# Seven block products for every fourth pair of row tiles in an MLP's second product

## The chip, the cores and the metric

The kernel runs on one core of one Trainium2 chip. The metric is the device time of one execution in microseconds (us). The engines are TensorE (PE in the profile; its weight loads PEld), VectorE (DVE), ScalarE (ACT), GpSimd (POOL) and SyncE (SP), which issues the DMAs. "fp32r" is the form in which TensorE takes 32-bit floats.

## The reference

One layer of an encoder over 256 tokens of width 2048: attention (GQA and MLA heads), attention to 256 memory tokens, and a squared-ReLU MLP, each followed by a layer norm of a scaled residual. What the change touches is the MLP at the end:

```python
def squared_relu_mlp(h, w_mlp_in, w_mlp_out):          # h (1, 256, 2048)
    return jnp.square(jax.nn.relu(h @ w_mlp_in)) @ w_mlp_out   # 2048 -> 8192 -> 2048
...
ff = squared_relu_mlp(x, w_mlp_in[l], w_mlp_out[l])
x = layer_norm(ALPHA * x + ff, ln3_g[l], ln3_b[l])
```

## The kernel before, in words

**Precision by three products.** Each operand is split into a high part (rounded, a copy on ScalarE, line 79) and a low part (the rest, a subtraction on VectorE, line 80), and a product is the sum of three matmuls: high x high, high x low, low x high (`mm3`, lines 144 to 147). `split` does this for weights and for activations alike.

**Weights.** A `Stream` takes a weight matrix in tiles of 1 MB: a buffer `raw` of 128 x 2048 (pool `rawp`, three buffers) is filled by one DMA from SP (line 133), and each half of it (1024 columns) is split into `w_hi` and `w_lo` (pool `wsp`, four buffers of each). After each half, `pump` issues a piece of waiting side work from the deque `side`.

**The MLP** (lines 703 to 760) walks over the 8192 hidden rows in NCH = 4 chunks of CH = 16 row tiles of 128. In a chunk:

- Four groups (`hidden_group`) of G = 4 row tiles make the hidden rows. The weights are the stationary operand and the tokens (`x2t`) move, so the result comes out transposed, rows by tokens. High weights multiply high and low tokens in one matmul of 512 columns (line 194), low weights the high tokens in one of 256 (line 199). A group reads eight halves, that is four `raw` tiles, and writes four PSUM banks, `acc` (pool `psA`, four banks) and `att` (pool `psT`, four banks) in turn. `hidden` (lines 706 to 712) adds the two halves of a bank, squares what is positive, and splits it into `ht`, which holds 16 tiles, each 256 high and 256 low columns.
- Then four column groups of 512 (`proj_tokens` on `s_mo`): for each of 16 tiles and each of two blocks of 128 tokens, one `mm3` with `ht` stationary and the weights moving. Each column group uses two banks, from `acc` for n = 0 and 1, from `att` for n = 2 and 3. At its end VectorE adds each bank to the rows of the residual, `res` (lines 755 and 758), and in the last chunk takes the statistics for the layer norm.
- The last column group of the last chunk has its weights split ahead into two wide buffers (`last_weights`, line 714) and runs token block by token block, so that the norm of the first block lies beside the matmuls of the second.

**Order.** The program is written in the order above, and the Tile framework's scheduler lays out each engine's queue at compile time; an instruction may go out ahead of earlier ones of the program when its inputs and its buffer are ready. Buffers are asked for by pool and name (`raw`, `w_hi`, `tmp`, `acc`). `big` is a pool of three buffers of 128 x 8192; in the MLP they hold `x2t`, and `ht` in turn, and the first group's weights, split early.

Of the kernel before, what the change touches and what calls it, by code (L numbers as in the profile page):

```python
# [11 lines left out]
F32 = mybir.dt.float32  # L12
F32R = mybir.dt.float32r
# [5 lines left out]
P = 128  # L19
# [19 lines left out]
def encoder_kernel(ctx: ExitStack, tc: tile.TileContext, t, out):  # L39
# [6 lines left out]
    midp = ctx.enter_context(tc.tile_pool(name="midp", bufs=1))  # L46
    resp = ctx.enter_context(tc.tile_pool(name="resp", bufs=2))
    tmp = ctx.enter_context(tc.tile_pool(name="tmp", bufs=7))
    ptp = ctx.enter_context(tc.tile_pool(name="ptp", bufs=2))
    small = ctx.enter_context(tc.tile_pool(name="small", bufs=6))  # L50
    psA = ctx.enter_context(tc.tile_pool(name="psA", bufs=4, space=bass.MemoryType.PSUM))
    psT = ctx.enter_context(tc.tile_pool(name="psT", bufs=4, space=bass.MemoryType.PSUM))

# [23 lines left out]
    def split(hi, lo, src, scale=None, pinned=False):  # L77
        if scale is None:
            pin(nc.scalar.activation(hi, src, AF.Copy), pinned)  # L79
            return pin(nc.vector.tensor_tensor(out=lo, in0=src, in1=f(hi), op=ALU.subtract), pinned)  # L80
# [413 lines left out]
    def stats_tile():  # L494
        return [small.tile([P, 5, 6], F32, tag="bn", name="bn"), 0]
# [210 lines left out]
    def hidden(ps, ht, j):  # L706
# [5 lines left out]
        split(ht[:, j, 0:S], ht[:, j, S:2 * S], lo)  # L712

    def last_weights(k):

        hi, lo = wide_w[0][:, k * 512:(k + 2) * 512], wide_w[1][:, k * 512:(k + 2) * 512]
        u, h = divmod(k, 4)
        if h == 0:
            wide_w[2] = raw_tile()
            nc.sync.dma_start(wide_w[2], t["w_mo"][s_mo.ap.shape[0] - 4 + u])  # L720
        split(hi, lo, wide_w[2][:, h * 512:(h + 2) * 512])
        return hi, lo

    G = 4

    def hidden_group(nexts, tiles, ht, j0):
# [7 lines left out]
        for i in range(G):  # L734
            hidden(outs[i], ht, j0 + i)

    for c in range(NCH):
        ht = big3(f"ht{c}")
        for g in range(CH // G):
            first = c == 0 and g == 0  # L740
            hidden_group((lambda k: w_mi0[k // 2]) if first else (lambda k: s_in.next()),
                         att_tile if g % 2 else acc_tile, ht, g * G)
            if first:
                side.extend(residual("ln2"))
        for n in range(4):
            tiles = att_tile if n >= 2 else acc_tile
            if c == NCH - 1 and n == 3:
                wide_w = [big.tile([P, 8192], F32R, tag="big", name=f"w{i}") for i in range(2)] + [None]
                ps = proj_tokens(None, ht, CH, 512, by_block=True, wide=last_weights, tiles=tiles)
            else:  # L750
                ps = proj_tokens(s_mo, ht, CH, 512, by_block=False, tiles=tiles)
            for b, o, w, p_ in ps:
                r = res[b][:, n * 512 + o:n * 512 + o + w]
                if c == 0:
                    nc.vector.scalar_tensor_tensor(out=r, in0=r, scalar=ALPHA, in1=p_[:, :w],
                                                   op0=ALU.mult, op1=ALU.add)
                else:
                    nc.vector.tensor_tensor(out=r, in0=r, in1=p_[:, :w], op=ALU.add)
                if c == NCH - 1:
                    stats(sts[b], r)  # L760

    g3, b3 = raw_tile(), raw_tile()
# [44 lines left out]
def _layout(i):  # L807
    f32 = np.float32
    a = {}
    x = np.asarray(i["x"])[0]  # L810
    a["x"] = x
    a["xT"] = np.ascontiguousarray(x.T.reshape(4, 4, P, S).transpose(0, 2, 1, 3)).reshape(4, P, 4 * S)
    a["mem"] = np.asarray(i["mem"])[0]
    w = np.asarray(i["w_in"])[0]
    qa, ka, va, cq, ckv, kr = np.split(w, np.cumsum([1024, 256, 256, 512, 512]), axis=1)
    a["w_qa"] = _rows(_pairs(qa, DH), 4, 512)
    a["w_ka"] = _rows(_pairs(ka, DH), 8, 256)
    a["w_vkr"] = _rows(np.concatenate([va, _pairs(kr, ROPE)], axis=1), 4, 320)
# [34 lines left out]
    a["w_mo"] = np.concatenate([_rows(mo[c * CH * P:(c + 1) * CH * P], 4, 512) for c in range(NCH)])  # L853
# [42 lines left out]
```

## Time and profile before

| | |
|---|---|
| median of 3 runs | 1123.22 us (1122.05 to 1123.25) |
| the profiled execution | 1123.25 us, of which the span from first to last instruction 1121.4 us |
| matmuls, TensorE busy | 6004, 1105.5 us (99%) |
| VectorE busy, ScalarE busy, GpSimd busy | 729.0 us (65%), 537.0 us (48%), 38.2 us (3%) |
| mean granted TensorE clock | 0.998 |
| DMA | 215.85 MB, mean 192 GB/s |
| the MLP's share | weights for the hidden rows and for the second product: 64 transfers of 1 MB each |

A row of a timeline reads: start in us from the start of the span, duration in us, engine, line of the kernel, operation, output <- inputs, count; in brackets the idle time of the engine ahead of it and who ended it. A row of the groups reads: line, engine, operation, output <- inputs, shapes, count | busy us in total, mean ns of one | idle us of the engine ahead of them and who ended it.

### The profile page before, as it was taken

The numbers are of one execution on the slowest core, as the hardware profiler recorded it, in microseconds if no ns is written. First come the engines' busy times: TensorE is split into PE (matmuls) and PEld (weight loads), VectorE is DVE, ScalarE is ACT, GpSimd is POOL, SyncE is SP. The second block draws the span as 40 slices with busy tenths as digits, with TensorE's granted clock in tenths as the row PEclk, the third lists the DMA queues.
The fourth block names the chain that finished last, engine by engine and source line by source line (L and its number), as shares of the span: only waits on it lengthen the run. The fifth ranks groups of instructions, "written<-read, shape, count | busy, mean of one in ns | idle before, by whom it ended". The sixth has DMA issues, their size and how long they took to land.

```text
span 1121.4 us, 15079 instructions
## 1 busy us (share of the span) xinstructions
PE 1105.5 (99%) x6004; PEld 954.2 (85%) x6004; DVE 729.0 (65%) x1036; ACT 537.0 (48%) x778; POOL 38.2 (3%) x45
## 2 busy tenths in 40 slices
PE   9999999999999989999999999999999999999996
PEld 6988899888998878888888888888888888888885
DVE  5878677687788677854545565555556454665575
ACT  6555565546576344543344454334444333544440
POOL 1402000000100000000000000000000000000000
PEclk9999999999999999999999999999999999999999
DMA  9664454476467426655555555555555555555562
GB/s 336 224 225 151 150 188 150 151 240 239 162 224 262 150 75 225 204 205 193 188 189 189 188 186 192 195 198 177 208 188 188 193 188 188 188 188 188 191 259 76
DMA packets 37942, 215.85 MB, mean 192 GB/s; under 512 B 4336, under 2 KB 5232, under 8 KB 14192
## 3 DMA queue, kind: packets, MB, share of 16 engines
q1 hardware_dynamic: 37872, 214.89, 54.6%
q8 instruction: 47, 0.77, 0.3%
q14 instruction: 23, 0.19, 0.1%
HBM read 212.78 MB, written 2.10 MB: 192 GB/s over the span
## 4 chain that ended last, share of the span: by engine, by line
PE 96%; DMA 2%; DVE 1%; ACT 0%; issue 0%; SPq 0%; POOL 0%; DVEq 0%; ACTq 0%
PE acc L146 12%; PE acc L145 12%; PE acc L147 12%; PE acc L194 11%; PE att L194 11%; PE att L147 6%; PE att L145 6%; PE att L146 6%; PE acc L199 5%; PE att L199 5%; PE acc L187 2%; PE acc L185 2%; PE acc L186 2%; PE att L534 1%; PE att L349 1%; DMA raw<-in_w_ka 1%
## 5 line engine op out<-in xcount | busy, mean ns | idle before, releaser
L80 DVE TENSOR_TENSOR w_lo<-raw,w_hi 128x1024 fp32r<-128x1024 f32 (+2 forms) x374 | 444.6, 1193 | 327.4 <-ACT w_hi L79 326.3
L79 ACT ACTIVATE w_hi<-raw 128x1024 fp32r<-128x1024 f32 (+2 forms) x374 | 386.5, 1036 | 459.0 <-PE acc L147 171.0
L194 PE MATMUL att<-x2t,w_hi 128*128 128x512 f32 x512 | 139.6, 394 | 0.0
L194 PE MATMUL acc<-x2t,w_hi 128*128 128x512 f32 x480 | 130.9, 394 | 0.0
L145 PE MATMUL acc<-w_hi,ht 128*128 128x512 f32 x256 | 99.6, 389 | 0.0
L146 PE MATMUL acc<-w_lo,ht 128*128 128x512 f32 x256 | 99.6, 389 | 0.0
L147 PE MATMUL acc<-w_hi,ht 128*128 128x512 f32 x256 | 99.6, 389 | 0.0
L194 PEld LDWEIGHTS att<-x2t,w_hi 128*128 128x128 f32 x512 | 88.1, 189 | 12.3
L194 PEld LDWEIGHTS acc<-x2t,w_hi 128*128 128x128 f32 x480 | 82.5, 189 | 11.5
L146 PE MATMUL att<-w_lo,ht 128*128 128x512 f32 x224 | 87.1, 389 | 0.0
L147 PE MATMUL att<-w_hi,ht 128*128 128x512 f32 x224 | 87.1, 389 | 0.0
L145 PE MATMUL att<-w_hi,ht 128*128 128x512 f32 x224 | 87.0, 389 | 0.0
L199 PEld LDWEIGHTS att<-x2t,w_lo 128*128 128x128 f32 x512 | 77.5, 189 | 10.2
L199 PEld LDWEIGHTS acc<-x2t,w_lo 128*128 128x128 f32 x480 | 72.6, 189 | 9.5
L199 PE MATMUL att<-x2t,w_lo 128*128 128x256 f32 x512 | 80.2, 281 | 0.0
L199 PE MATMUL acc<-x2t,w_lo 128*128 128x256 f32 x480 | 75.1, 281 | 0.0
L146 PE MATMUL acc<-w_lo,xt 128*128 128x512 f32 (+2 forms) x192 | 69.5, 363 | 0.2 <-DVE w_lo L80 0.2
L147 PE MATMUL acc<-w_hi,xt 128*128 128x512 f32 (+2 forms) x192 | 69.1, 361 | 0.0
L145 PE MATMUL acc<-w_hi,xt 128*128 128x512 f32 (+2 forms) x192 | 66.1, 364 | 1.0 <-ACT w_hi L79 1.0
L147 PEld LDWEIGHTS acc<-w_hi,ht 128*128 128x128 f32 x256 | 48.0, 188 | 10.0
L145 PEld LDWEIGHTS acc<-w_hi,ht 128*128 128x128 f32 x256 | 48.0, 188 | 10.0
L146 PEld LDWEIGHTS acc<-w_lo,ht 128*128 128x128 f32 x256 | 48.0, 188 | 10.0
(221 smaller groups left out, 1738.1 us busy)
## 6 DMA issues: line engine op xcount, KB each, us to landing
raw<-in_w_mi SPq DMA_DIRECT2D x64, 1024.0 KB, 4.8
raw<-in_w_mo SPq DMA_DIRECT2D x64, 1024.0 KB, 4.8
raw<-in_w_out SPq DMA_DIRECT2D x16, 1024.0 KB, 4.9
raw<-in_w_b SPq DMA_DIRECT2D x5, 1024.0 KB, 4.8
raw<-in_w_qa SPq DMA_DIRECT2D x16, 256.0 KB, 5.4
raw<-in_w_qa SPq DMA_DIRECT2D x4, 1024.0 KB, 4.9
raw<-in_w_ckv SPq DMA_DIRECT2D x4, 1024.0 KB, 5.1
raw<-in_w_cq SPq DMA_DIRECT2D x4, 1024.0 KB, 4.8
```

What stands on the lines that cost most here:

```text
L79: pin(nc.scalar.activation(hi, src, AF.Copy), pinned)
L80: return pin(nc.vector.tensor_tensor(out=lo, in0=src, in1=f(hi), op=ALU.subtract), pinned)
L145: nc.tensor.matmul(ps, ah, bh, start=start, stop=False)
L146: nc.tensor.matmul(ps, ah, bl, start=False, stop=False)
L147: nc.tensor.matmul(ps, al, bh, start=False, stop=stop)
L185: nc.tensor.matmul(ps, hi, xt[:, k, 0:S], start=k == 0, stop=False)
L186: nc.tensor.matmul(ps, hi, xt[:, k, S:2 * S], start=False, stop=False)
L187: nc.tensor.matmul(ps, lo, xt[:, k, 0:S], start=False, stop=k == nk - 1)
L194: nc.tensor.matmul(ps, hi[:, i * P:(i + 1) * P], xt[:, k, :], start=k == 0, stop=k == nk - 1)
L199: nc.tensor.matmul(ps[:, 0:S], lo[:, i * P:(i + 1) * P], xt[:, k, 0:S], start=False, stop=False)
L349: nc.tensor.transpose(pp[:, st * S + b * P:st * S + b * P + P], ev[:, b, st * P:(st + 1) * P], ident)
L534: nc.tensor.transpose(ps[:, o:o + P], x(b, k // 4)[:, (k % 4 + j) * P:(k % 4 + j + 1) * P], ident)
```

## The change

The second product is now made in blocks: two column groups at a time (half q of the 2048 columns), all 16 row tiles of the chunk, both token blocks. So a chunk has two blocks, each with four `acc` banks x11, x12, x21, x22 (token block, column group) and, new, four `att` banks p1, p5, p6, p7. The row tiles go in eight pairs p. Three pairs of four are multiplied as before: 2 tiles x 2 token blocks x 2 column groups x 3 matmuls. For p = 3 and p = 7, the 2 x 2 blocks (tokens by row tiles, row tiles by columns) are multiplied by the Strassen-Winograd scheme with seven products in place of eight. For that

- `hidden` also forms four sums of 128 x 128 blocks of hidden values, on VectorE, and splits them (`sums_h`);
- `load_unit` loads the weights of a pair (1 MB as before, laid out so that the four blocks lie side by side), and for p = 3 and 7 puts three additions on VectorE (`sums_w`) on `side`. Units of p = 0, 1, 4, 5 lie in `raw` buffers, the others in the third `big` buffer (`wx`), whose use becomes possible since `ht` is now one buffer for all chunks. Units are asked for two ahead; the first two of a chunk just before its last hidden group;
- at the end of a block the seven products are put together in `res`: four additions of the x banks, four with the p banks, and four more on VectorE (q = 0) or GpSimd (q = 1), and one copy on ScalarE.

The second half of the columns in the last chunk stays as it was. The pools `midp` and `ptp`, no longer needed there, are closed ahead of the MLP to make room for `sums_h`.

```diff
-    s_in, s_mo = Stream(t["w_mi"][4:]), Stream(t["w_mo"])
+    early.close()
+    late = ctx.enter_context(tc.tile_pool(name="late", bufs=1))
+    s_in = Stream(t["w_mi"][4:])
     sts = [stats_tile() for _ in range(NB)]
+    ht = big3("ht")
+    sums_h = late.tile([P, 2048], F32R, name="sums_h").rearrange("p (u l c) -> p u l c", l=2, c=512)
+    wx = big.tile([P, 8192], F32, tag="big", name="wx")
+    raw2, sums_w = [[wx[:, o:o + 2048] for o in (i, i + 2048)] for i in (0, 4096)]
...
+    def hidden(ps, j):
+        r = []
+        for i in range(2):
+            r.append(square(ps[i]))
+            split(ht[:, j + i, 0:S], ht[:, j + i, S:2 * S], r[i])
+        if strassen(j // 2):
+            (a11, a21), (a12, a22) = [(x[:, 0:P], x[:, P:S]) for x in r]
+            s = tmp_tile()
+            s1, s2, s3, s4 = [s[:, o:o + P] for o in range(0, 4 * P, P)]
+            for o, a, b, op in ((s1, a21, a22, ALU.subtract), (s3, a11, a21, ALU.subtract),
+                                (s2, s1, a11, ALU.subtract), (s4, a12, s2, ALU.add)):
+                nc.vector.tensor_tensor(out=o, in0=a, in1=b, op=op)
+            split(sums_h[:, j // 8, 0, :], sums_h[:, j // 8, 1, :], s)
+
+    def strassen(p):
+        return p % 4 == 3
...
+    def load_unit(chunk):
+        if not units or units[0][0] != chunk:
+            return
+        c, q, p = units.pop(0)
+        seven = strassen(p)
+        raw = raw_tile() if p % 4 < 2 else raw2[p % 4 - 2]
+        nc.sync.dma_start(raw, t["w_mo"][(c * 2 + q) * (CH // 2) + p])
+        s = None
+        if seven:
+            s = sums_w[p // 4 % 2]
+            b12, b22, b21 = [raw[:, o:o + 512] for o in (0, 1024, 1536)]
+            def add(out, a, b):
+                side.append(lambda: nc.vector.tensor_tensor(out=out, in0=a, in1=b, op=ALU.add))
+            add(s[:, 0:1024]..., raw[:, 512:1536]..., b12[:, None, :].broadcast_to([P, 2, 512]))
+            add(s[:, 1024:1536], s[:, 0:512], b22)
+            add(s[:, 1536:2048], s[:, 1024:1536], b21)
+        loaded.append((raw, s))
...
+    def pair_product(c, q):
+        x11, x12, x21, x22 = [acc_tile() for _ in range(4)]
+        p1, p5, p6, p7 = [att_tile() for _ in range(4)]
+        n = CH // 2
+        for p in range(n):
+            load_unit(c)
+            raw, s = loaded.popleft()
+            k = 2 * p
...
+            if strassen(p):
+                first, last = p == 3, p == n - 1
+                pump(len(side))
+                for src, todo in ((raw[:, 512:1536], ((p1, a(k, 0), first), (x12, sm(3), False))),
+                                  (raw[:, 1536:2048], ((x11, a(k + 1, 0), False),)),
+                                  (s[:, 0:1024], ((p5, sm(0), first), (p7, sm(2), first))),
+                                  (s[:, 1024:2048], ((p6, sm(1), first), (x21, a(k + 1, 1), False)))):
+                    for (hi, lo), (ps, (ah, al), start) in zip(part(src), todo):
+                        mm3(ps, ah, al, hi, lo, start, last)
+            else:
+                for i in range(2):
+                    w = part(raw[:, i * 1024:(i + 1) * 1024])
+                    for (hi, lo), to in zip(w, ((x12, x22), (x11, x21))):
+                        for b in range(2):
+                            ah, al = a(k + i, b)
+                            mm3(to[b], ah, al, hi, lo, p == 0 and i == 0, to[b] is x22 and p == n - 2 and i == 1)
...
+        rest = nc.gpsimd if q == 1 else nc.vector
+        first_add(r22, x22)
+        m1 = tmp_tile()
+        nc.scalar.activation(m1, p1, AF.Copy)
+        first_add(r12, x12)
+        first_add(r11, x11)
+        add(r12, r12, p5)
+        add(r22, r22, p5)
+        u3 = tmp_tile()
+        u2 = tmp_tile()
+        add(u2, m1, p6)
+        add(u3, u2, p7)
+        first_add(r21, x21)
+        add(r11, r11, m1, eng=rest)
+        add(r12, r12, u2, ALU.subtract, rest)
+        add(r21, r21, u3, eng=rest)
+        add(r22, r22, u3, ALU.subtract, rest)
...
     for c in range(NCH):
-        ht = big3(f"ht{c}")
         for g in range(CH // G):
             first = c == 0 and g == 0
+            if g == CH // G - 1:
+                load_unit(c)
+                load_unit(c)
             hidden_group((lambda k: w_mi0[k // 2]) if first else (lambda k: s_in.next()),
-                         att_tile if g % 2 else acc_tile, ht, g * G)
+                         att_tile if g % 2 else acc_tile, g * G)
...
-        for n in range(4):
-            tiles = att_tile if n >= 2 else acc_tile
...
+        for q in range(2):
+            if c < NCH - 1 or q == 0:
+                pair_product(c, q)
+                continue
```

`part` splits 512 or 1024 columns of a source into `w_hi` and `w_lo` and pumps one piece of side work; `first_add(r, ps)` adds a bank to the residual rows (scaled by ALPHA in the first chunk).

More of the change, by code (lines that the diff above doesn't have):

```diff
@@ L724, in encoder_kernel, with hidden_group @@
     G = 4
-    def hidden_group(nexts, tiles, ht, j0):
+    def hidden_group(nexts, tiles, j0):
         outs = [tiles() for _ in range(G)]
@@ L733, in hidden_group @@
                           x2t, k + i, KT)
-        for i in range(G):
-            hidden(outs[i], ht, j0 + i)
+        for i in range(0, G, 2):
+            hidden(outs[i:i + 2], j0 + i)
+    units = [(c, q, p) for c in range(NCH) for q in range(2) for p in range(CH // 2)
+             if not (c == NCH - 1 and q == 1)]
+    loaded = deque()
+    def load_unit(chunk):
[11 more added lines that the diff above has]
+                side.append(lambda: nc.vector.tensor_tensor(out=out, in0=a, in1=b, op=ALU.add))
+            add(s[:, 0:1024].rearrange("p (i c) -> p i c", i=2), raw[:, 512:1536].rearrange("p (i c) -> p i c", i=2),
+                b12[:, None, :].broadcast_to([P, 2, 512]))
+            add(s[:, 1024:1536], s[:, 0:512], b22)
+            add(s[:, 1536:2048], s[:, 1024:1536], b21)
+        loaded.append((raw, s))
@@ new lines, in part, with a, sm, first_add @@
+    def part(src):
+        w = src.shape[1]
+        hi = wsp.tile([P, 1024], F32R, tag="w_hi", name="w_hi")
+        lo = wsp.tile([P, 1024], F32R, tag="w_lo", name="w_lo")
+        split(hi[:, :w], lo[:, :w], src)
+        pump()
+        return [(hi[:, o:o + 512], lo[:, o:o + 512]) for o in range(0, w, 512)]
+    def pair_product(c, q):
[6 more added lines that the diff above has]
+            k = 2 * p
+            def a(k_, b):
+                return ht[:, k_, b * P:(b + 1) * P], ht[:, k_, S + b * P:S + (b + 1) * P]
+            def sm(i):
+                return (sums_h[:, p // 4, 0, i * P:(i + 1) * P], sums_h[:, p // 4, 1, i * P:(i + 1) * P])
+            if strassen(p):
[14 more added lines that the diff above has]
+                            mm3(to[b], ah, al, hi, lo, p == 0 and i == 0, to[b] is x22 and p == n - 2 and i == 1)
+        cols = [slice((2 * q + i) * 512, (2 * q + i + 1) * 512) for i in range(2)]
+        r11, r12, r21, r22 = [res[b][:, cc] for b in range(NB) for cc in cols]
+        def first_add(r, ps):
+            if c == 0:
+                nc.vector.scalar_tensor_tensor(out=r, in0=r, scalar=ALPHA, in1=ps,
+                                               op0=ALU.mult, op1=ALU.add)
+            else:
+                nc.vector.tensor_tensor(out=r, in0=r, in1=ps, op=ALU.add)
+        def add(o, x, y, op=ALU.add, eng=nc.vector):
+            eng.tensor_tensor(out=o, in0=x, in1=y, op=op)
+        rest = nc.gpsimd if q == 1 else nc.vector
[15 more added lines that the diff above has]
+        add(r22, r22, u3, ALU.subtract, rest)
+        if c == NCH - 1:
+            for b, r in ((0, r11), (0, r12), (1, r21), (1, r22)):
+                stats(sts[b], r)
@@ new lines, in encoder_kernel @@
+        for q in range(2):
+            if c < NCH - 1 or q == 0:
+                pair_product(c, q)
+                continue
+            s_ml = Stream(t["w_ml"])
+            for n in (2, 3):
+                if n == 3:
+                    wide_w = [big.tile([P, 8192], F32R, tag="big", name=f"w{i}") for i in range(2)] + [None]
+                    ps = proj_tokens(None, ht, CH, 512, by_block=True, wide=last_weights, tiles=att_tile)
+                else:
+                    ps = proj_tokens(s_ml, ht, CH, 512, by_block=False, tiles=acc_tile)
+                for b, o, w, p_ in ps:
+                    r = res[b][:, n * 512 + o:n * 512 + o + w]
@@ L852, in _layout @@
     mo = np.asarray(i["w_mlp_out"])[0]
-    a["w_mo"] = np.concatenate([_rows(mo[c * CH * P:(c + 1) * CH * P], 4, 512) for c in range(NCH)])
+    m = mo.reshape(NCH, CH // 2, 2, P, 2, 2, 512)
+    order = [m[:, :, i, :, :, j, :] for i, j in ((0, 1), (0, 0), (1, 1), (1, 0))]
+    m = np.stack(order, axis=4).transpose(0, 3, 1, 2, 4, 5).reshape(NCH * CH, P, 2048)
+    a["w_mo"] = m[:-CH // 2]
+    a["w_ml"] = _rows(mo[-CH * P:, 1024:], 4, 512)
     for n in ("ln1", "ln2", "ln3", "mem_ln"):
```

22 lines of the change are left out of this document (6 added, 16 removed).

## The prediction

> **What bounds the kernel now.** I read the head of the page first (span, engines), then the chain that ended last, then stretches of the MLP and its groups of instructions, because the change lies there.
>
> ```profile
> span 1121.4 us, 15079 instructions
> PE 1105.5 (99%) x6004; PEld 954.2 (85%) x6004; DVE 729.0 (65%) x1036; ACT 537.0 (48%) x778; POOL 38.2 (3%) x45
> PE 96%; DMA 2%; DVE 1%; ACT 0%; issue 0%; SPq 0%; POOL 0%; DVEq 0%; ACTq 0%
> 624.72:647.16 22.44, 22.44 (x130) 19.63 (x128) 13.72 (x21) 10.93 (x17) 0.00 (x0) 1.00 0.53 189
> 669.60:756.50 86.90, 86.90 (x385) 71.97 (x384) 46.71 (x51) 35.91 (x39) 0.00 (x0) 1.00 0.55 190
> 669.60 0.39 PE L145 MATMUL acc<-w_hi,ht 128*128 128x512 f32 x1
> 756.64 1.07 PE L194 MATMUL acc<-x2t,w_hi 128*128 128x512 f32 x4
> L80 DVE TENSOR_TENSOR w_lo<-raw,w_hi 128x1024 fp32r<-128x1024 f32 x350 | 427.3, 1223 | 323.9 <-ACT w_hi L79 323.1
> L79 ACT ACTIVATE w_hi<-raw 128x1024 fp32r<-128x1024 f32 x350 | 370.7, 1061 | 448.2 <-PE acc L147 165.1 <-PE att L147 82.9 <-PE acc L194 82.5
> ```
>
> The profiled execution took 1123.25 us (span 1121.4), the median of the three is 1123.22, so they are the same. TensorE is the chain: 96% of it. The two stretch rows (the first number after the window is its length, then busy time and count of PE, PEld, DVE, ACT, POOL) are a group of hidden rows and a chunk's second product: PE is busy for all of both, at clock 1.00. Behind PE there is slack that waits on PE itself: the weight splits on ScalarE (448.2 us idle, mostly until PE gives back a split buffer) and VectorE. The second product of a chunk runs from 669.60 to 756.64: 16 k x 2 token tiles x 4 column groups x 3 = 384 matmuls, so one costs 87.04/384 = 0.2267 us. A cut of matmuls is worth its full price as long as weights and PSUM banks still come in time.
>
> **The change part by part.** *Fewer matmuls.* The code makes 4 chunks x 2 column halves x 8 pairs, less the last half: 7 blocks, each with two pairs (p = 3 and 7) by seven products. Such a pair needs 7 x 3 = 21 matmuls in place of 24. 14 x 3 x 0.2267 = **9.5 us saved**.
>
> *More work on VectorE, ScalarE, GpSimd.* The prices, and one place where GpSimd adds beside VectorE:
>
> ```profile
> L565 DVE TENSOR_TENSOR res<-res,tmp 128x512 f32<-128x512 f32 x32 | 20.6, 685 | 1.4 <-DMA tmp<-in_ln_g 1.1 <-DMA tmp<-in_ln_b 0.2
> 1066.44 1.28 DVE L758 TENSOR_TENSOR res<-res,acc 128x512 f32<-128x512 f32 x2
> L295 DVE TENSOR_TENSOR tmp<-acc,tab_a 128x128 f32<-128x128 f32 x4 | 1.0, 282 | 0.0
> 32.51 1.30 POOL L297 TENSOR_TENSOR tmp<-tmp 128x512 f32<-128x512 f32 x1 [6.72 <-DVE tmp L295]
> 34.37 4.96 POOL L297 TENSOR_TENSOR tmp<-tmp 128x512 f32<-128x512 f32 x1 [0.55 <-DVE rs_v L88]
> 34.34 3.82 DVE L80 TENSOR_TENSOR w_lo<-raw,w_hi 128x1024 fp32r<-128x1024 f32 x4
> ```
>
> Weight sums: one add of 1024 and two of 512, 1.22 + 2 x 0.68 = 2.6 us a pair, 14 times: 36 us. Splits: 3.5 parts of 1024 in place of 2, so 1.5 x 1.22 x 14 = 26 us on VectorE and 22 us on ScalarE. Sums of hidden rows: 8 times four adds of 128 (0.28 each) and a split of 512 (0.68): 14 us. Results: 12 adds a block in place of 4 (in three blocks four of them go to GpSimd): 44 more x 0.68 = 30 us. VectorE comes to 729 + 106 = 835 us, 74% of the span. Averaged, all of it lies in the idle time of the L80 row, and I cost the weight sums, the hidden sums and the splits at nothing: they are issued two units ahead and the four split buffers let them run 4 parts ahead of PE. The ends of the blocks are another matter (below). GpSimd's 12 adds (1.3 to 5.0 us each) feed rows of the result that are next needed two products later: nothing.
>
> *Loads moved ahead.* As many transfers of 1 MB are issued as before (56 + 8), but the first two units of each chunk are asked for ahead of the last hidden group's four weight tiles, and they sit in two of the three raw buffers until the second product begins. This is the step that I price highest:
>
> ```profile
> 147.87 6.98 SPq L133 DMA_DIRECT2D raw<-in_w_out  x2
> 172.52 4.97 SPq L133 DMA_DIRECT2D raw<-in_w_out  x2
> 191.87 37.49 SPq L133 DMA_DIRECT2D raw<-in_w_out  x7
> 229.41 10.41 SPq L593 DMA_DIRECT2D tmp<-in_mem  x10
> 210.16 0.46 ACT L338 ACTIVATE tmp<-att,nm 128x256 f32<-128x256 f32 x1
> 229.64 0.47 ACT L338 ACTIVATE tmp<-att,nm 128x256 f32<-128x256 f32 x1
> 628.22 0.33 SPq L133 DMA_DIRECT2D raw<-in_w_mi  x1
> 632.44 0.33 SPq L133 DMA_DIRECT2D raw<-in_w_mi  x1
> 638.06 0.33 SPq L133 DMA_DIRECT2D raw<-in_w_mi  x1
> raw<-in_w_mi SPq DMA_DIRECT2D x64, 1024.0 KB, 4.8
> DMA to landing us min/median/max: 3.5/4.8/9.7
> 1070.06 0.33 SPq L720 DMA_DIRECT2D raw<-in_w_mo  x1
> 1074.91 2.01 ACT L79 ACTIVATE w<-raw 128x1024 fp32r<-128x1024 f32 x2 [1.49 <-DMA raw<-in_w_mo]
> 1076.01 2.36 DVE L80 TENSOR_TENSOR w<-raw,w 128x1024 fp32r<-128x1024 f32 x2 [1.33 <-ACT w L79]
> 1078.40 0.33 SPq L720 DMA_DIRECT2D raw<-in_w_mo  x1
> 582.78 0.93 PE acc L194 x4
> ```
>
> Could the scheduler let the group's tiles pass the two units? The first rows speak against it. The mem loads need only a tmp buffer and stand in the program behind the eighth w_out tile, yet eleven (2 + 2 + 7) went out before them; they went at 229.41, beside the last attention exponentials (229.64) that take tmp buffers, though none had taken one since 210.16. So buffers of one name seem to be handed out in program order, and only different names pass each other. Then U0 and U1 take the buffers that come free at 628.22 and 632.44, and the group's first tile goes out at 638.06. From there one buffer turns round: issue 1070.06, data used from 1074.91, both halves split, issued again 1078.40, 8.34 us a turn, with the first half ready 7.1 us after issue (1076.01 + 1.18). A group of 22.44 us eats one tile in 5.61 us. The fourth tile's first half is ready at 638.06 + 3 x 8.34 + 7.1 = 670.2; PE, starting the group at 647.16 (end of the window above), wants its low half, after four high matmuls (0.93), at 647.16 + 3 x 5.61 + 0.9 = 664.9. PE is late by **5.3 us a chunk, 21.2 us for four**. Ends: at the shortest landing (3.5, not 4.85) four landings are 5.4 us shorter and nothing is lost; at transfers half again as slow it is 10 us a chunk. I take 5.3, because 4.8 is the median of 64 such transfers.
>
> *Ends of the blocks.* Before, a product wrote two banks and the next had two others. Now all four acc banks end with the block, x21 with its very last matmul, and the next work writes the same four. Within a block's last pair (21 x 0.2267 = 4.8 us) and up to the second part of the next block (12 matmuls, 2.7 us later) VectorE must do one split left over (1.22), eight adds that empty banks (at 0.64 back to back, the L758 row of two), and two splits (2.44): 8.8 us in 7.5, so 1.3 us late. Four blocks end this way (three first halves, and the last one, ahead of the old product). Where a hidden group follows (three times), bank x21 is wanted at 3 x 0.23 = 0.7 us, and VectorE has emptied it after u2, u3 and the add, 1.2 us if at once, 2.5 us with a split between: 1.2 us late in the mean. 4 x 1.3 + 3 x 1.2 = **8.8 us**. The trace of before has no such end; the bounds are nothing (VectorE takes the reads early, PE does other banks first) and all adds ahead of the next split: 1.22 + 12 x 0.64 + 1.22 = 10.1 us from 4.4 us before the end, 5.5 us late, with eight adds 2.9: 4 x 5.5 + 3 x 2.9 = 31 us. I take the lower value, since in the rows above splits start as soon as ScalarE is done.
>
> GpSimd's adds at three block ends share something with VectorE: the add took 1.30 us alone and 4.96 us while four splits ran, and those four took 3.82 us together, 0.96 each, no more than the 1.22 of the L80 row. The one that waits is GpSimd, so I cost VectorE nothing. The Trainium skill (SBUF — State Buffer, section "SBUF: two separate sides") says that a GpSimd instruction and a VectorE one with two SBUF inputs take one port pair as an exclusive lock, and whichever starts first holds it for its whole length. The trace agrees for GpSimd; by the rule VectorE could be the one that waits, up to 1.3 us for each of four adds, and the sum would be up to 15.6 us higher.
>
> *Kept.* The last half stays as it was; its wide buffers now wait for the block before it instead of the hidden group, which ends some 22 us (one old product) before 1083, while their first data come at 1074.91: nothing.
>
> **Sum:** 1123.25 - 9.5 + 21.2 + 8.8 = **1143.7 us**.
>
> **The rivals.** *A, faster: no starvation.* If weight tiles of the last hidden group pass the two units, or a unit is split early and gives its buffer back, the 21.2 us vanish, and if PE at the block ends does other banks first, half of their price too. For it: the split buffers have slack that a scheduler could use. Against it: the w_out and mem rows. Then 1123.25 - 9.5 + 8.8 / 2 = 1118; it decides when PE's lateness in the last hidden group is under (9.5 - 4.4) / 4 = 1.3 us a chunk. *B, VectorE's order.* All adds ahead of the splits at the block ends: 31 in place of 8.8, 1166. For it, they stand first in the program; against it, they wait for PE one by one, and splits fit between. *C, the lock of the port pair turned against VectorE* at the three ends: 4 x 1.3 x 3 = 15.6, up to 1159. Against it: the four splits at 34.34. *D, the change pays for itself and no more:* landings near 3.5 us leave no starvation, and the block ends take back 8.8 of 9.5: 1122.5, with 1119 to 1127 for a little of either. For it: the shortest landing; against it: the 4.8 is of a stage with one transfer at a time, as here.
>
> **How the numbers follow.** Forecast 0.55 (its own range 1128 to 1160); A 0.19 (0.17 faster, 0.02 no difference); B 0.10; C 0.05; D 0.11 (0.02 faster, 0.06 no difference, 0.03 slower). Faster by over 0.2% (about 2.2 us, what a measurement here can tell from no change) 0.19, within it 0.08, slower 0.73. The range that holds 8 in 10 goes from 1117, to take in most of A and D, to 1160, above C and the upper part of the forecast, without B.
>
> **What would show it.** Right: 42 matmuls fewer in the second product, at 0.227 us start to start; in each chunk's last hidden group, idle PE of some 2.5 us twice, with ACT w_hi waiting for DMA raw<-in_w_mi, and issues of w_mi there 8 us apart instead of 5.6; at the block ends PE waiting 1 to 2 us for DVE res or w_lo; VectorE at 73 to 75%. Wrong: issues of w_mi staying 5.6 us apart there (then A); PE gaps of 5 us at block ends with DVE res first (then B); VectorE's splits stretched beside GpSimd's adds (then C).

## The result, and the profile after

The changed kernel takes 1151.78 us (median of 4 runs, 1148.94 to 1155.82) against 1123.09 us: ratio 1.026, 95% interval 1.0229 to 1.0292, slower. Forecast were 1143.7 us (1117 to 1160) and "slower" with 0.73. The profiled execution took 1151.52 us. First the head of its page and its chain that ended last:

```profile
span 1149.7 us, 15234 instructions
PE 1114.6 (97%) x5962; PEld 951.6 (83%) x5962; DVE 821.7 (71%) x1190; ACT 563.5 (49%) x821; POOL 62.1 (5%) x57
PE 80%; DMA 10%; DVE 5%; ACT 2%; issue 2%; SPq 0%; POOL 0%; ACTq 0%; DVEq 0%; POOLq 0%
```

TensorE does 42 matmuls fewer, as meant, yet is busy 9.1 us *longer* (1114.6 for 1105.5), and the chain, 96% TensorE before, now has 10% DMA and 5% VectorE in it. Two readings follow from this: TensorE waits, and some of its matmuls are slower or drawn out. What it waits for (us in total, times, longest):

```profile
PE att L195 <- ACT w_hi L80: 15.6, 10, 2.9
PE acc L147 <- DVE w_lo L81: 2.2, 4, 0.6
PE acc L200 <- DVE w_lo L81: 1.9, 3, 0.6
```

L195 into att is the matmul of a chunk's last hidden group (and its second); L147 and L200 into acc are the first uses of low weights behind a block's end. Now the stretches, read as the row 624.72 to 647.16 of before: first a chunk's third hidden group, in 22.44 us, then the last groups of the four chunks, from the start of each to the start of its second product.

```profile
447.95:470.39 22.44, 22.44 (x129) 19.63 (x128) 16.64 (x31) 9.43 (x15) 0.00 (x0) 1.00 0.67 229
470.39:501.22 30.83, 25.12 (x117) 20.40 (x116) 15.94 (x23) 11.89 (x18) 0.00 (x0) 0.89 0.37 126
657.68:685.59 27.91, 23.66 (x117) 19.13 (x116) 12.91 (x20) 11.31 (x16) 0.00 (x0) 0.94 0.36 119
842.16:868.45 26.29, 22.90 (x117) 19.02 (x116) 12.91 (x20) 11.29 (x16) 0.00 (x0) 0.94 0.38 127
1025.01:1051.22 26.21, 23.35 (x118) 19.12 (x116) 12.92 (x20) 11.30 (x16) 0.00 (x0) 0.93 0.38 126
```

The last groups are long, by 3.8 to 8.4 us within these stretches, with the DMA share down from 0.67 to 0.37 and the clock (the column ahead of it) at 0.89 to 0.94. That is not the whole loss: the last twelve of a group's 128 matmuls stand behind the first four of the second product, as here in the third chunk:

```profile
868.45 1.07 PE L146 MATMUL acc<-w_hi,ht 128*128 128x512 f32 x4
869.36 1.11 PE L200 MATMUL att<-x2t,w_lo 128*128 128x256 f32 x8
870.32 1.09 PE L195 MATMUL att<-x2t,w_hi 128*128 128x512 f32 x4
```

Counted to the end of its own matmuls (871.25 here, where the next one starts), less the 0.91 us of those four, a group loses 10.3, 7.4, 5.7 and 5.7 us in the four chunks, 29.0 us in all.

Inside the second chunk's group, the requests for weights and ScalarE's splits (start, duration, in brackets the idle time before and who ended it):

```profile
643.16 0.33 SPq L782 DMA_DIRECT2D raw<-in_w_mo  x1
648.59 27.20 SPq L134 DMA_DIRECT2D raw<-in_w_mi  x4
653.52 2.01 ACT L80 ACTIVATE w_hi<-raw 128x1024 fp32r<-128x1024 f32 x2 [6.22 <-DMA raw<-in_w_mi]
663.59 2.01 ACT L80 ACTIVATE w_hi<-raw 128x1024 fp32r<-128x1024 f32 x2 [2.44 <-DMA raw<-in_w_mi]
671.98 2.01 ACT L80 ACTIVATE w_hi<-raw 128x1024 fp32r<-128x1024 f32 x2 [6.37 <-DMA raw<-in_w_mi]
```

The `w_mo` request at 643.16 and one before it hold two of three raw buffers; the four `w_mi` requests go out one by one, the last ending 27.20 us after the first, so (27.20 - 0.33)/3 = 8.96 us a turn on the average. The second turn alone took 10.07 us: its tile was asked for at 657.00 and ScalarE could start on it only 6.6 us later, at 663.59, where the first tile took 4.9 us. The page shows the waits in the idle time of `ACT w_hi`, ended by DMA each time, and one step later as TensorE's wait for `w_hi`.

What the wait leaves behind is seen in the third chunk. TensorE's first matmuls behind a gap (timeline), and three stretches, the first in that gap:

```profile
855.91 2.07 PE L195 MATMUL att<-x2t,w_hi 128*128 128x512 f32 x4 [2.22 <-ACT w_hi L80]
```

```profile
853.69:855.64 1.95, 0.00 (x0) 0.00 (x0) 0.00 (x0) 0.84 (x1) 0.00 (x0) 1.00 0.12 50
855.64:859.05 3.41, 3.14 (x9) 2.67 (x10) 2.36 (x2) 1.16 (x2) 0.00 (x0) 0.50 0.00 0
859.05:862.50 3.45, 3.45 (x20) 3.01 (x19) 0.00 (x0) 0.00 (x0) 0.00 (x0) 1.00 0.87 304
```

Four matmuls take 2.07 us instead of about 1.09. The granted clock is still 1.00 for the first 1.95 us of the gap, 0.50 for the next 3.41 us, then 1.00 again. Five such stretches lie in the last hidden groups. By an estimate (5 x 3.41 / 2) they make 8.5 us of TensorE's extra busy time, which is about half of it: 42 matmuls fewer should have left 1105.5 - 9.5 = 1096.0 us, and `e1_late` below, which has no such stretch in the MLP, is still busy for 1101.7 us.

Last, VectorE at a block's end (second chunk, q = 0), and the wait of TensorE that it makes:

```profile
724.61 0.68 DVE L844 TENSOR_TENSOR res<-res,acc 128x512 f32<-128x512 f32 x1
725.87 1.23 DVE L789 TENSOR_TENSOR wx<-wx 128x1024 f32<-128x1024 f32 x1 [0.58 <-DMA wx<-in_w_mo]
727.01 1.22 DVE L81 TENSOR_TENSOR w_lo<-wx,w_hi 128x1024 fp32r<-128x1024 f32 x1
728.15 0.68 DVE L844 TENSOR_TENSOR res<-res,acc 128x512 f32<-128x512 f32 x1
728.75 0.69 DVE L789 TENSOR_TENSOR wx<-wx 128x512 f32<-128x512 f32 x1
729.35 0.68 DVE L844 TENSOR_TENSOR res<-res,acc 128x512 f32<-128x512 f32 x1
729.95 1.22 DVE L81 TENSOR_TENSOR w_lo<-raw,w_hi 128x1024 fp32r<-128x1024 f32 x1
731.23 0.50 PE L147 MATMUL acc<-w_lo,ht 128*128 128x512 f32 x1 [0.64 <-DVE w_lo L81]
```

The split at 729.95 is the one TensorE needs to open the next block. Two weight sums (L789) of a pair that is multiplied some 17 us later stand ahead of it, and VectorE even idled 0.58 us for the transfer that feeds the first.

### The profile page after: what moved, and what is told of

It reads as the page before. It is cut to its first block, busy times and chain, and to the rows that moved or that the text cites. A ratio compares the mean times of both kernels' runs of the same rounds, so it can differ in the third digit from the quotient of the medians.

```text
span 1149.7 us, 15234 instructions
## 1 busy us (share of the span) xinstructions
PE 1114.6 (97%) x5962; PEld 951.6 (83%) x5962; DVE 821.7 (71%) x1190; ACT 563.5 (49%) x821; POOL 62.1 (5%) x57
## 4 chain that ended last, share of the span: by engine, by line
PE 80%; DMA 10%; DVE 5%; ACT 2%; issue 2%; SPq 0%; POOL 0%; ACTq 0%; DVEq 0%; POOLq 0%
PE acc L147 14%; PE acc L148 14%; PE acc L146 14%; PE acc L195 8%; PE att L195 7%; DMA raw<-in_w_mi 6%; PE acc L200 4%; PE att L200 4%; DVE w_lo L81 3%; PE acc L188 2%; PE acc L186 2%; PE acc L187 2%; DMA wx<-in_w_mo 2%; ACT w_hi L80 2%; PE att L146 2%; PE att L148 2%
## 5 line engine op out<-in xcount | busy, mean ns | idle before, releaser
L81 DVE TENSOR_TENSOR w_lo<-raw,w_hi 128x1024 fp32r<-128x1024 f32 (+2 forms) x318 | 376.7, 1202 | 190.6 <-ACT w_hi L80 184.0
L80 ACT ACTIVATE w_hi<-raw 128x1024 fp32r<-128x1024 f32 (+2 forms) x318 | 321.8, 1030 | 321.7 <-PE acc L148 85.7
L195 PE MATMUL att<-x2t,w_hi 128*128 128x512 f32 x512 | 145.4, 407 | 15.6 <-ACT w_hi L80 15.6
L147 PE MATMUL acc<-w_lo,ht 128*128 128x512 f32 x396 | 155.1, 392 | 1.9 <-DVE w_lo L81 1.9
L148 PE MATMUL acc<-w_hi,ht 128*128 128x512 f32 x396 | 154.2, 389 | 0.0
L80 ACT ACTIVATE w_hi<-wx 128x1024 fp32r<-128x1024 f32 x84 | 82.6, 991 | 134.3 <-PE acc L148 130.6
L81 DVE TENSOR_TENSOR w_lo<-wx,w_hi 128x1024 fp32r<-128x1024 f32 x84 | 94.6, 1136 | 64.7 <-ACT w_hi L80 64.7
L195 PE MATMUL acc<-x2t,w_hi 128*128 128x512 f32 x480 | 133.7, 395 | 0.0
L146 PE MATMUL acc<-w_hi,ht 128*128 128x512 f32 x396 | 130.7, 390 | 0.0
L195 PEld LDWEIGHTS att<-x2t,w_hi 128*128 128x128 f32 x512 | 91.4, 196 | 30.5 <-ACT w_hi L80 17.7
L195 PEld LDWEIGHTS acc<-x2t,w_hi 128*128 128x128 f32 x480 | 82.5, 189 | 12.1 <-DVE res L844 0.5
L200 PEld LDWEIGHTS att<-x2t,w_lo 128*128 128x128 f32 x512 | 79.7, 196 | 15.0 <-DVE w_lo L81 5.2
L147 PEld LDWEIGHTS acc<-w_lo,ht 128*128 128x128 f32 x396 | 74.3, 188 | 20.6 <-DVE w_lo L81 5.3
L146 PEld LDWEIGHTS acc<-w_hi,ht 128*128 128x128 f32 x396 | 74.3, 188 | 15.9 <-DVE res L844 0.4
L148 PEld LDWEIGHTS acc<-w_hi,ht 128*128 128x128 f32 x396 | 74.3, 188 | 15.2
L200 PE MATMUL att<-x2t,w_lo 128*128 128x256 f32 x512 | 84.4, 291 | 0.6
L200 PEld LDWEIGHTS acc<-x2t,w_lo 128*128 128x128 f32 x480 | 73.0, 189 | 14.0 <-DVE w_lo L81 5.3
L200 PE MATMUL acc<-x2t,w_lo 128*128 128x256 f32 x480 | 78.9, 283 | 1.9 <-DVE w_lo L81 1.9
L147 PE MATMUL acc<-w_lo,xt 128*128 128x512 f32 (+2 forms) x192 | 69.3, 362 | 0.3 <-DVE w_lo L81 0.3
L146 PE MATMUL acc<-w_hi,xt 128*128 128x512 f32 (+2 forms) x192 | 66.0, 363 | 0.9 <-ACT w_hi L80 0.9
L847 POOL TENSOR_TENSOR res<-res,tmp 128x512 f32<-128x512 f32 x12 | 23.8, 1998 | 548.5 <-DVE res L844 342.9
```

The lines of the kernel that those rows point to most:

```text
L146: nc.tensor.matmul(ps, ah, bh, start=start, stop=False)
L147: nc.tensor.matmul(ps, ah, bl, start=False, stop=False)
L148: nc.tensor.matmul(ps, al, bh, start=False, stop=stop)
L195: nc.tensor.matmul(ps, hi[:, i * P:(i + 1) * P], xt[:, k, :], start=k == 0, stop=k == nk - 1)
L200: nc.tensor.matmul(ps[:, 0:S], lo[:, i * P:(i + 1) * P], xt[:, k, 0:S], start=False, stop=False)
L847: eng.tensor_tensor(out=o, in0=x, in1=y, op=op)
```

## The experiments

Theory: most of the loss is the two units asked for ahead of the last hidden group, which hold raw buffers; the rest is at the block ends. Rivals: the block form itself (four banks that end together), the clock, or GpSimd beside VectorE. "Late" below means the diff of `e1_late`.

**e1_late: the units asked for behind the group.**

```diff
         for g in range(CH // G):
-            if g == CH // G - 1:
-                load_unit(c)
-                load_unit(c)
             hidden_group(...)
+            if g == CH // G - 1:
+                load_unit(c)
+                load_unit(c)
```

> The changed kernel, with the first two units of each chunk asked for behind the last hidden group instead of ahead of it. Theory (two of three raw buffers are held while the group's four weight tiles need them): the last hidden group is back at 22.4 us in all four chunks, the issues of w_mi in it are 5.6 us apart again, and the half-clock windows of the MLP go; about 30 us of the 40 lost vanish and the block ends stay: 1120 to 1123 us. Rival (the loss is VectorE's added work): the groups get a little shorter at most and the time stays above 1140.

Measured: 1122.49 us, ratio 0.9993 (0.9984 to 1.0003). The last hidden group is back at

```profile
470.39:492.83 22.44, 22.44 (x129) 19.62 (x128) 13.72 (x21) 10.93 (x17) 0.00 (x0) 1.00 0.56 191
```

and no half-clock stretch is left in the MLP. 29.3 us hang on where two requests stand. At six of the seven block ends TensorE still loses some 1.5 us each: its next matmul starts about 1.1 us behind the one ahead of it, where 0.23 is usual, and a few more come late. The 9.5 us of matmuls saved are nearly all given back there. The seventh end, that of the last chunk, has no gap; no weight sum for a next block stands there.

**e2_one: one unit early, one late.**

```diff
             if g == CH // G - 1:
                 load_unit(c)
-                load_unit(c)
             hidden_group(...)
+            if g == CH // G - 1:
+                load_unit(c)
```

> The changed kernel with one unit of each chunk asked for ahead of the last hidden group, the other behind it. Theory: with two raw buffers turning at 8.4 us each, a tile comes every 4.2 us, less than the 5.6 that PE needs, so nothing starves: within 2 us of the kernel with both behind it, 1120 to 1124. Rival (every unit asked for early costs its share): half way, 1134 to 1138.

Measured: 1122.51 us, 0.9997 (0.9987 to 1.0007). Two free buffers are enough; it is the second held buffer that costs everything.

**e3_hold: the kernel before, with nothing but the hold.**

```diff
+            if g == CH // G - 1:
+                s_mo.ahead()     # asks for the next w_mo tile into a raw buffer
+                s_mo.ahead()
             hidden_group(...)
```

> The kernel before, changed in one thing: the first two tiles of w_mo of each chunk are asked for ahead of the last hidden group. Theory: this alone costs what the last hidden groups lost in the changed kernel, 24 to 31 us: 1147 to 1154. Rival (the loss needs the new blocks): under 1130.

Measured: 1150.3 us, 1.0249 (1.0229 to 1.0269). The same wait stands first among TensorE's waits, and, in the stretch below it, the second chunk's last group, which starts at 655.97 here, has nearly the length and the clock of the changed kernel's (27.91 us, 0.94):

```profile
PE att L201 <- ACT w_hi L79: 18.6, 11, 2.3
```

```profile
655.97:683.68 27.71, 23.12 (x117) 19.11 (x116) 13.73 (x21) 11.27 (x16) 0.00 (x0) 0.94 0.41 138
```

The hold alone, in a kernel without blocks and without seven products, costs 27.2 us.

**e4_eight: blocks, late, but eight products in every pair.**

```diff
     def strassen(p):
-        return p % 4 == 3
+        return False
```

(with the p banks and their adds dropped.)

> The kernel with both units behind the group, and all pairs multiplied by eight products: no sums, no p banks, four adds at a block's end. It has 42 matmuls (9.5 us) more than the changed kernel. Theory (the block ends cost because VectorE has 12 adds and the weight sums there): ends nearly free, 1123 to 1126. Rival (they cost because all four acc banks end together): the ends keep their 8 us, 1129 to 1133.

Measured: 1123.09 us, 0.9997 (0.9988 to 1.0006), and not one gap of TensorE in the MLP. Four banks that end together and are claimed again at once cost nothing when VectorE has only four adds to do there. One of them goes ahead of the split (VectorE's timeline, second chunk, q = 0), the other three behind it:

```profile
710.75 0.69 DVE L834 TENSOR_TENSOR res<-res,acc 128x512 f32<-128x512 f32 x1 [1.08 <-PE acc L148]
711.35 1.22 DVE L81 TENSOR_TENSOR w_lo<-raw,w_hi 128x1024 fp32r<-128x1024 f32 x1
```

So the block ends of the changed kernel must be made by what VectorE does besides: weight sums or p adds.

**e5_pool: late, with the weight sums on GpSimd.**

```diff
-                side.append(lambda: nc.vector.tensor_tensor(out=out, in0=a, in1=b, op=ALU.add))
+                side.append(lambda: nc.gpsimd.tensor_tensor(out=out, in0=a, in1=b, op=ALU.add))
```

> The kernel with both units behind the group, with the 42 weight sums on GpSimd instead of VectorE. Theory 1 (sums for the next block's unit run as soon as its data land, at the block ends, 2.6 us of VectorE ahead of the split that PE waits for): the gaps at the block ends shrink from 1.5 and 1.1 us to under 0.5, 1116 to 1119. Theory 2 (the 12 adds and the last bank alone make the ends late): no change, 1121.5 to 1123.5. Rival (the port pair's lock makes VectorE wait for GpSimd's long adds): VectorE's splits are stretched and it gets slower, above 1125.

Measured: 1131.97 us, 1.0071 (1.0058 to 1.0085), 9.5 us above e1_late. The rival came true: VectorE's splits wait beside GpSimd's adds, and TensorE for them (L147 for `DVE w_lo`, 5.1 us into `att` and 3.7 us into `acc`). One place of the timeline:

```profile
690.51 6.86 POOL L789 TENSOR_TENSOR wx<-wx 128x1024 f32<-128x1024 f32 x3 [95.83 <-DMA wx<-in_w_mo]
690.83 3.15 DVE L81 TENSOR_TENSOR w_lo<-wx,w_hi 128x1024 fp32r<-128x1024 f32 x1 [1.50 <-ACT w_hi L80]
693.91 4.54 DVE L81 TENSOR_TENSOR w_lo<-raw,w_hi 128x1024 fp32r<-128x1024 f32 x2
694.04 0.50 PE L147 MATMUL att<-w_lo,sums_h 128*128 128x512 f32 x1 [0.32 <-DVE w_lo L81]
```

A split that takes 1.22 us took 3.15 us, two took 4.54 us, while three adds ran 6.86 us on GpSimd. That is the mechanism of the prediction's rival C, in another place and at a price that TensorE pays.

**e6_mid: late, with the seven-product pairs at p = 2 and 6**, the p banks put into the result during p = 7, and the x adds last.

```diff
-        return p % 4 == 3
+        return p % 4 == 2
...
+                if last:            # p = 6
+                    combine()       # the p banks into res
...
+        for r, ps in ((r12, x12), (r22, x22), (r11, x11), (r21, x21)):
+            add(r, r, ps)
```

> The kernel with both units behind the group, with the seven-product pairs at p = 2 and 6 instead of 3 and 7, and the p banks put into the result during p = 7, so that only four adds remain at a block's end. Same matmuls, same adds, sums on VectorE. Theory 2 (adds and the last bank make the ends late): gaps of 0.2 us at most, 1113.5 to 1116. Theory 1 (the weight sums do): they come at another time but as eagerly, so about half remains, 1117 to 1120.

Measured: 1149.07 us, 1.0235 (1.0221 to 1.0249). A miss for the theory. The gaps grew to 2.8 and 3.2 us; TensorE waits for `DVE res` 11.5 us with L146 and 9.2 us with L195. A block end (second chunk, q = 0) in the timeline:

```profile
718.10 2.36 DVE L81 TENSOR_TENSOR w_lo<-raw,w_hi 128x1024 fp32r<-128x1024 f32 x2
720.37 0.69 DVE L820 TENSOR_TENSOR res<-res,acc 128x512 f32<-128x512 f32 x1
721.21 0.77 PE L146 MATMUL acc<-w_hi,ht 128*128 128x512 f32 x1 [2.76 <-DVE res L820]
```

Two splits, for later matmuls of the next block, stand ahead of the add that gives back the bank, and TensorE stops at that bank. With the p adds taken first, on the same rows of the result, the x adds had become the last work of the block. 0.77 us for the first matmul shows half clock here, too.

**e7_warm: the changed kernel with TensorE kept busy in the gaps.** Eight matmuls of 512 bf16 columns on a constant ahead of the third and the fourth tile of each last hidden group.

```diff
         for k in range(0, KT, 2):
+            if j0 == CH - G and k in (8, 12):
+                warm()
             hi, lo = nexts(k)
```

> The changed kernel (units ahead of the group, starving), with eight matmuls on constants put ahead of the third and the fourth weight tile of each last hidden group, where PE would stand idle 2.3 us; their result is not used. They are to keep the clock up. Theory (the stage waits for data, so a halved clock loses little): 1149 to 1153. Rival (each half-clock window of 3.4 us costs 1.7 us, five of them): 1142 to 1146.

Measured: 1146.96 us, 1.0209 (1.0193 to 1.0224), 4.8 us below the changed kernel and between what the two theories expected. The starvation remains, part of its aftermath goes: in the profiled execution (1152.10 us, the slowest of its four) the last groups of chunks two to four have no stretch at half clock. That all of the 4.8 us is the clock is not shown. Counted as above, these three groups lose 5.5 to 5.7 us; in the changed kernel the third and the fourth, each with such a stretch, lost 5.7, because the next wait for weights took it up, and the second lost more for its late tile.

**e8_mid_pool: e6_mid and e5_pool in one.**

> Both: seven-product pairs at p = 2 and 6, and the weight sums on GpSimd. If either theory of the block ends is the whole, as good as the better of the two; if both have a part, better than each: 1113.6 (all of the 9.5 us) to 1116. With the lock: slower than the one with sums on VectorE.

Measured: 1169.46 us, 1.0416 (1.0401 to 1.0431), slower than either alone, as the expectation had it for the lock: the waits of both are in it (`DVE res` 12.6 and 9.2 us, `DVE w_lo` 8.6 and 4.9 us).

**e9_mid_x: late, pairs at p = 2 and 6, the four x adds first and all on VectorE, the p work behind them.** It leaves out the layer-norm statistics of the last chunk's four pieces of q = 0 (23 of 27 such instructions run, some 2.5 us of VectorE).

```diff
+        for r, ps in ((r12, x12), (r22, x22), (r11, x11), (r21, x21)):
+            first_add(r, ps)
+        for x in ((u2, m1, p6), (u3, u2, p7), (r12, r12, p5), (r22, r22, p5), ...):
+            side.append(...)        # one beside each following split
```

> The block's last two units are asked for behind the last hidden group, the seven-product pairs are p = 2 and 6, and at the end of a block VectorE adds the four x banks to the result first; the p banks, which nothing claims for another 11 us or more, follow one by one beside the splits of the next unit, all on VectorE. Theory: the six gaps of 1.15 to 1.5 us at the block ends come from VectorE's order there (weight sums and p adds ahead of a split), so with only four x adds at the end, which left no gap in the form with eight products throughout, they go: 1122.5 - 8.9 = 1113.6, and 1113 to 1116 is expected. Rival: eight more adds a block, all of VectorE, delay the splits of the next unit instead: 1118 to 1123.

Measured: 1129.82 us, 1.0056 (1.0042 to 1.0069). Another miss, for both. The timeline at the same block end:

```profile
712.15 0.68 DVE L847 TENSOR_TENSOR tmp<-tmp,att 128x512 f32<-128x512 f32 x1
712.75 1.22 DVE L81 TENSOR_TENSOR w_lo<-raw,w_hi 128x1024 fp32r<-128x1024 f32 x1
713.89 2.48 DVE L844 TENSOR_TENSOR res<-res,acc 128x512 f32<-128x512 f32 x4
714.72 0.47 PE L146 MATMUL acc<-w_hi,ht 128*128 128x512 f32 x1 [2.05 <-DVE res L844]
```

Against e4_eight, where one x add went ahead of the split, all four stand behind it here, and the first bank comes back some 2 us late at six block ends (a seventh gap, of 1.8 us, is a late split at p = 2). The place of one split among the adds decides, and the scheduler had put it differently. "Four adds at the end are free" holds only for the order that e4_eight happened to have.

**e10_no_sums: late, with the weight sums left out** (the products that should take sums take the weights themselves); the adds stay as in e1_late.

```diff
-            s = sums_w[p // 4 % 2]
-            ...                     # three additions on VectorE
+            s = raw
```

> The form with the late loads and the seven-product pairs at p = 3 and 7, with the weight sums left out: the products that should take sums take the weights themselves. The adds at the block end are as before. If the weight sums that VectorE does there, ahead of the split that TensorE waits for, make the gaps, the gaps shrink from 1.15 to 1.5 us to under 0.5 us and the time is 1114 to 1117. If the x and p adds alone make them, the gaps stay and the time is 1121 to 1123.

Measured: 1114.55 us, 0.9925 (0.9911 to 0.9938). The gaps are gone but for 0.1 us over the usual 0.23 at three block ends. All x and p adds are still there, so the sums make the block ends' loss, by their work or by their place.

**e11_pinned: late, with each weight sum held in the order of the program**, the whole computation in it.

```diff
-                side.append(lambda: nc.vector.tensor_tensor(out=out, in0=a, in1=b, op=ALU.add))
+                side.append(lambda: pin(nc.vector.tensor_tensor(out=out, in0=a, in1=b, op=ALU.add), True))
```

> Both repairs in one, with the whole computation: the block's first two units are asked for behind the last hidden group, and each weight sum is held behind the instruction that stands before it on VectorE in the order of the program, so that none is put between the last splits of a block and the split that opens the next. Theory: what the form without the sums gained, 1123.1 - 8.5 = 1114.6, is kept, since the 42 sums (36.3 us of VectorE in all) now lie beside products that leave VectorE idle: 1114 to 1117. Rival: held in order, a sum whose weights have not landed blocks VectorE and the splits behind it, and the gaps move into the blocks: 1118 to 1130.

Measured: **1114.43 us, ratio 0.9921 (0.9907 to 0.9934)**: faster than both kernels. Engines and chain of its page, and VectorE's timeline at the same block end:

```profile
PE 1098.2 (99%) x5962; PEld 949.4 (85%) x5962; DVE 823.0 (74%) x1190; ACT 564.8 (51%) x821; POOL 57.9 (5%) x57
PE 98%; DVE 1%; DMA 0%; issue 0%; POOL 0%; ACT 0%; DVEq 0%; SPq 0%; POOLq 0%
```

```profile
707.31 1.28 DVE L844 TENSOR_TENSOR res<-res,acc 128x512 f32<-128x512 f32 x2
708.50 1.22 DVE L81 TENSOR_TENSOR w_lo<-raw,w_hi 128x1024 fp32r<-128x1024 f32 x1
709.64 1.28 DVE L847 TENSOR_TENSOR res<-res,att 128x512 f32<-128x512 f32 x2
710.84 1.22 DVE L81 TENSOR_TENSOR w_lo<-raw,w_hi 128x1024 fp32r<-128x1024 f32 x1
711.97 0.68 DVE L847 TENSOR_TENSOR res<-res,tmp 128x512 f32<-128x512 f32 x1
712.57 0.68 DVE L847 TENSOR_TENSOR tmp<-tmp,att 128x512 f32<-128x512 f32 x1
713.17 1.22 DVE L81 TENSOR_TENSOR w_lo<-raw,w_hi 128x1024 fp32r<-128x1024 f32 x1
714.31 1.22 DVE L789 TENSOR_TENSOR wx<-wx 128x1024 f32<-128x1024 f32 x1
```

VectorE has as many instructions as after the change (1190) and as much to do; the first sum now comes behind three splits of the next block. 8.7 of the 9.5 us that 42 matmuls are worth arrive. So it was the sums' place, not their work.

**e12_after_pinned: the changed kernel, its early requests kept, with the same pin.**

> The changed kernel as it is, its two early requests for weights kept, with the weight sums alone held in the order of the program. Theory: the two losses are independent, so the time falls by the 8 us of the block ends and the loss in the last hidden groups stays: 1151.8 - 8 = 1144, 1142 to 1146. Rival: the early requests bring the sums of the first block of a chunk forward and so have a part in the gaps at the block ends, or the sums' order has a part in the starved groups: the time stays at 1148 or above, or falls below 1140.

Measured: 1143.2 us, 1.0182 (1.0164 to 1.02), as the theory said. The account closes in two independent steps: the order of the sums 1151.8 - 1143.2 = 8.6 us, the early requests 1143.2 - 1114.4 = 28.8 us.

## Why the prediction was right in sign, and 8 us short

- **Fewer matmuls, 9.5 us saved:** right. 5962 for 6004, and e11_pinned gains 8.7 us.
- **Loads moved ahead, 21.2 us lost:** the mechanism was right, the term too small: 28.8 and 29.3 us by two pairs of runs, 29.0 by the four groups above (10.3, 7.4, 5.7 and 5.7 us where 5.3 each was forecast). Buffers of one name were indeed handed out in program order, so rival A fell. In the second chunk the first request came at 648.59; the row of before gives 638.06 + (657.68 - 647.16) = 648.58. Where no tile came late, in the third and the fourth chunk, the forecast for a group is met within 0.4 us, and the turn is (25.55 - 0.33)/3 = 8.41 us in the third, for 8.34 in the working:

```profile
833.06 25.55 SPq L134 DMA_DIRECT2D raw<-in_w_mi  x4
```

  The step that was mis-sized is "5.3 us a chunk, 21.2 us for four", one undisturbed group taken for all. In the second chunk one tile came late and made a turn of 10.07 us. In the first, the first request came at 463.60, where the row of before gives 638.06 + (470.39 - 647.16) = 461.29; the three turns were 1.0 us longer together; and a stretch at half clock lay behind the last wait, where nothing takes it up (1.7 us, an estimate from 3.41 / 2). Why that request came late no run separates. The half clock was not in the working, which had every matmul at 0.2267 us; its price is that 1.7 us by this trace, and at most the 4.8 us of e7_warm by the medians; how much of the 4.8 it is stays open.
- **Ends of the blocks, 8.8 us:** 8.1 us (e1_late to e11_pinned) and 8.6 us (the changed kernel to e12_after_pinned) measured, for another reason; that the sizes agree is luck. The step that failed is "I cost the weight sums ... at nothing". The working priced the adds that empty eight banks and three splits; e10_no_sums, with all of those, shows next to no loss, and e11_pinned shows that the sums are free where they stand behind the splits. The working also put 1.3 us on the last chunk's end, where VectorE has all 12 adds and no weight sum; no gap is there. "Issued two units ahead" was true, and it was the harm: with the weights there early, the scheduler put the sums early, into the tightest 7 us of VectorE. Two errors met, adds priced too high and sums at nothing.
- **Rival B, all adds ahead of the splits:** not in the changed kernel. e6_mid and e9_mid_x show the same kind of loss reversed, splits ahead of adds, at 2 to 3 us an end.
- **Rival C, the lock of the port pair:** it did turn against VectorE in the changed kernel, and cost TensorE nothing that the runs show. Beside GpSimd's 12 adds (L847, 2.0 us in the mean) six splits of 1024 columns took 1.72 to 2.32 us in place of 1.22, as here:

```profile
778.56 2.20 POOL L847 TENSOR_TENSOR res<-res,tmp 128x512 f32<-128x512 f32 x1 [2.46 <-DVE tmp L847]
780.12 1.73 DVE L81 TENSOR_TENSOR w_lo<-raw,w_hi 128x1024 fp32r<-128x1024 f32 x1
```

  e11_pinned has six such splits too (1.72 to 1.85 us) and no gap of TensorE behind them; the MLP of the kernel before and of e4_eight, without adds on GpSimd, has none. With 42 sums on GpSimd in e5_pool TensorE does pay. The Trainium skill (SBUF — State Buffer, section "SBUF: two separate sides") has the one that starts first hold the pair for its whole instruction. The traces agree: the split above ends 1.09 us after the add that began ahead of it, and a split takes 3.15 us in e5_pool behind an add that began 0.32 us earlier. The row of before was no proof against it: its four splits, 0.96 us in the mean, were two of 1024 columns at 1.22 and two of 640 at 0.81, and the add had begun 0.03 us behind the first of them.
- **Rival D, 1122.5 us:** the form that gives this time is e1_late, by taking the starvation away, not by short landings.
- **VectorE at 73 to 75%:** 821.7 us for the 835 worked out; 71% only since the span is longer.

## What to carry to other kernels

A load asked for earlier is not free: it takes a buffer from a stream that turns through the same few, so count the buffers left and divide the turn by them (here 8.4 us a tile on one buffer against 5.6 us needed; with two buffers nothing was lost). An engine at 71% on the average can still be the bound for 7 us at a seam; work with slack that is ready early must be held back behind the urgent instruction there, and holding 42 sums in the order of the program was worth 8.1 to 8.6 us. Test two repairs one at a time and together: either alone left the kernel no faster than before, and only both showed the gain.

## What the runs showed of the hardware that was not expected

- Half clock after short gaps: TensorE idled 2.22 us ahead of 855.91, and the clock went to half 1.95 us into that gap, for 3.41 us. The Trainium skill (TensorE: Matmul & The Clock Gate, section "What's actually happening") states half speed after at least one idle window of about 3.4 us and full speed after a busy one of about that length; the length of the slow stretch agrees, the idle time needed was shorter here. It did not follow every time: of seven gaps of about 2 us in e9_mid_x two were followed by it, of seven gaps of 2.1 to 2.3 us in e3_hold four.
- VectorE's splits beside GpSimd's adds: 1.22 us alone, 1.72 to 2.32 us for six in the changed kernel, 3.15 us for one and 4.54 us for two in e5_pool.
